# Grouping the RWKV output products behind the state products, with a two-bank PSUM tile

## The chip, the cores and the metric

The kernel runs on one core of a Trainium2 chip. The metric is the device time of one execution in microseconds (us); of several runs the median is given. The engines are named as the profile names them: PE (TensorE, matmul; PEld is its weight load), DVE (VectorE), ACT (ScalarE), POOL (GpSimd) and SP (SyncE, which only issues transfers here). Matmul results land in PSUM, which has eight banks of 512 f32 in each of 128 partitions.

## The reference, cut to what matters

One layer of a hybrid encoder: a normalised input goes through one projection into three head groups (Mamba-2 SSD, RWKV-7, memory cross-attention), whose outputs are joined, projected, normalised and added to the input. Sequence 4096, width 1024, all f32. The change lies in the RWKV group, four heads of 64:

```python
def rwkv7_recurrence(r, w, k, v, a_vec, b_vec):
    """S_t = S_{t-1} (diag(w_t) + a_t^T b_t) + v_t^T k_t ; y_t = S_t r_t."""
    ...

def rwkv7_group(u, mu, w0, w2, a0, a2, k_k, k_a, r_k, lnx_w, lnx_b):
    prev = jnp.pad(u, ((0, 0), (1, 0), (0, 0)))[:, :l, :]
    us = (u + (prev - u) * mu).astype(jnp.float32)        # token shift
    r, k, v, g = ...                                      # 256 columns each, then two low-rank inputs
    ...
    y = rwkv7_recurrence(rh, hs(decay), kh, vh, -kk, kk * ah)
    mean = jnp.mean(y, axis=-1, keepdims=True)
    var = jnp.mean(jnp.square(y - mean), axis=-1, keepdims=True)
    y = (y - mean) * lax.rsqrt(var + LNX_EPS)
    ...
    return ((y + bonus).reshape(b, l, W) * jax.nn.silu(g)).astype(u.dtype)
```

## The kernel before

The kernel has three phases: `phase_a` (SSD group, to about 800 us of the span), `phase_b` (RWKV group, about 800 to 1610 us) and `phase_c` (cross-attention and output projection). In each the sequence is cut into 16 pieces of 256 tokens; this text calls the work on one piece in phase B a round. Matrix products of the projections are split into high and low parts, so each takes three matmuls a block of 128 inputs (`proj_cm`, L143).

In phase B several generators are traced in turn by `weave`, which gives each a share: `stage1` of piece i (projections and what is made of them), `gram2` and `solve2` of piece i-1, `stage3` and `stage4` of piece i-2. Each `yield` hands over to the next generator. The order of tracing is the priority; a planner with its own timing model then lays the instructions of each engine in order, taking among those that are ready the one traced first. `tc.high_priority(offset=n)` treats what is traced inside as if it had been traced n places earlier; `tc.issue_after(x)` lets nothing traced inside go ahead of x on x's engine. The engines then run their instructions in the planned order, with semaphores between engines.

- `shifted` projects a block pair into the PSUM tile `ps_pj` (two of these), and evicts it with the token shift: ACT scales by 1-mu into `tt` (L583), DVE adds mu times the column before (L584), POOL puts the last token of the piece before into column 0 (L586, from `cm`), and DVE writes the new last token into `cm` (L587). There are nine blocks in five calls a round.
- `gram2` makes four 128x128 products for each of two heads, twice a round (L746), into the PSUM banks `ps_yd` and `ps_st`, and DVE evicts each bank under a mask into `AT` (L749). In the last round the banks `ps_g` and `ps_tr` are used.
- `solve2` inverts 64x64 triangular blocks, with small matmuls (L801, L809, L821, L831); `nct` (L762, L769) is an intermediate of it, `N` the next.
- `tokmaj` copies v, the scaled b and k, `rr` (the scaled r, L856, ACT) and `el` (L857, POOL) of the next piece into the layouts that `stage3` reads.
- `stage3` runs four chunks of 64 tokens, one after the other. A chunk copies the state `ST` into `UV` (L887), multiplies (L894), copies to `X` (L897), multiplies (L901), copies to `UV` (L906), multiplies into the state's update (L911) and adds it (L914); `S0` is the decayed state (L889, POOL). After each second chunk the output products of both are made: from `rr` and the states (L928), and from `AT` and `UV` (L931), into the banks `ps_yd` and `ps_st` again. These are f32 products on 64 rows or columns (64x64 and 128x64 shapes of the array); the profile counts two matmuls for each.
- `stage4` takes mean (L943), difference (L947) and variance of the outputs, transposes them back, and writes the piece to DRAM.

The order in which TensorE gets the output products is thus the planner's: a product may go as soon as its inputs are there.

## Time and profile before

| what | value |
|---|---|
| time, median of 3 runs | 2216.97 us (2215.18 to 2217.18) |
| the profiled execution | 2213.0 us, its span 2211.3 us, granted TensorE clock 0.99 |
| PE busy | 2151.4 us, 97% |
| DVE / ACT / POOL busy | 1502.5 (68%) / 1184.0 (54%) / 721.5 us (33%) |
| DMA | 97 GB/s over the span |
| one round of phase B in its steady part | 46.6 us |

A row of the timeline has the start in us from the beginning of the span, the duration in us, the engine, the line, the operation, what is written and read (by the program's tile names), the form, and how many alike were merged. For a matmul the form gives the part of the array that is used (rows x columns), then what streams through. Rows of groups have a count after x, busy us in all, the mean ns of one, and after the bar the idle time of that engine just before them, with what ended it.

### The profile page before, as it was taken

Reading aid. Unit: us, or ns where it says so; the run is one execution under the profiler, and the core shown is the slowest. Engines: PE = TensorE matmul, PEld = TensorE weight load, DVE = VectorE, ACT = ScalarE, POOL = GpSimd, SP = SyncE. Lnnn points to the kernel's source line nnn. Section 1 sums busy time; section 2 is a strip of 40 time slices with the busy share of each in tenths; the row PEclk is TensorE's granted clock in tenths of the full one; section 3 lists DMA queues with packets and bytes.
Section 4 is the critical chain, followed back from the end, with each engine's and each line's share of the span. In section 5 each row is a group of like instructions: output and inputs, shape, how many; then the busy total and the mean of one; then the engine's idle time right before and its main releaser. Section 6 shows DMA issues by size and latency. Waiting matters only on the chain.

```text
span 2211.3 us, 51042 instructions
## 1 busy us (share of the span) xinstructions
PE 2151.4 (97%) x20705; PEld 1980.4 (90%) x20705; DVE 1502.5 (68%) x3438; ACT 1184.0 (54%) x2877; POOL 721.5 (33%) x1043
## 2 busy tenths in 40 slices
PE   6999999999999889999999999999999999999998
PEld 6999999999999888899899998898888888888986
DVE  6788878888888886577776777777664444444452
ACT  7555555555554565566666666677643333333441
POOL 1334344343443343233334334333112212222223
PEclk9999999999999999999999999999999999999999
DMA  6332223322233331112111121123253324333232
GB/s 206 128 113 96 87 96 123 117 96 92 94 137 120 108 96 40 44 45 83 49 45 45 45 80 47 49 73 135 92 189 117 133 102 162 110 130 133 101 124 77
DMA packets 83610, 218.86 MB, mean 99 GB/s; under 512 B 9191, under 2 KB 45486, under 8 KB 71086
## 3 DMA queue, kind: packets, MB, share of 16 engines
q1 hardware_dynamic: 81294, 215.56, 27.9%
q8 instruction: 163, 2.67, 0.5%
q14 instruction: 73, 0.60, 0.1%
q10 hardware_dynamic: 2080, 0.04, 0.1%
HBM read 152.00 MB, written 63.57 MB: 97 GB/s over the span
## 4 chain that ended last, share of the span: by engine, by line
PE 85%; DMA 5%; DVE 5%; ACT 3%; issue 1%; POOL 1%; POOLq 0%; SPq 0%; ACTq 0%; DVEq 0%
PE ps_pj L143 40%; PE ps_pj L153 8%; PE ps_yd L153 8%; PE ps_st L153 7%; DMA w_st<-in_w_in_dram 1%; DVE cc L312 1%; PE ps_yd L441 1%; PE ps_yd L746 1%; PE ps_pj L1159 1%; PE ps_tr L132 1%; PE ps_yo L894 1%; PE ps_yo L901 1%; PE ps_tr L1147 1%; PE ps_st L433 1%; PE ps_yo L911 1%
## 5 line engine op out<-in xcount | busy, mean ns | idle before, releaser
L143 PE MATMUL ps_pj<-hh,w_hi 128*128 128x256 f32 x2704 | 792.6, 293 | 13.4 <-ACT w_hi L80 3.8
L143 PE MATMUL ps_pj<-hh,w_lo 128*128 128x256 f32 x2704 | 780.9, 289 | 1.6 <-DVE w_lo L81 1.6
L143 PE MATMUL ps_pj<-hl,w_hi 128*128 128x256 f32 x2704 | 778.8, 288 | 0.0
L143 PEld LDWEIGHTS ps_pj<-hh,w_hi 128*128 128x128 f32 x2704 | 521.0, 193 | 25.9 <-ACT w_hi L80 7.3
L143 PEld LDWEIGHTS ps_pj<-hh,w_lo 128*128 128x128 f32 x2704 | 520.7, 193 | 8.5 <-DVE w_lo L81 2.6
L143 PEld LDWEIGHTS ps_pj<-hl,w_hi 128*128 128x128 f32 x2704 | 521.1, 193 | 6.8
L312 DVE SCALAR_TENSOR_TENSOR cc<-ux,cwh,cc 128x256 f32<-128x256 f32 x384 | 218.0, 611 | 11.4 <-ACT cc L309 11.0
L153 PE MATMUL ps_pj<-w_hi,hh 128*128 128x260 f32 (+1 forms) x528 | 153.5, 291 | 4.8 <-ACT hh L135 4.0
L153 PE MATMUL ps_pj<-w_hi,hl 128*128 128x260 f32 (+1 forms) x528 | 150.9, 286 | 0.0
L153 PE MATMUL ps_pj<-w_lo,hh 128*128 128x260 f32 (+1 forms) x528 | 149.9, 284 | 0.0
L1166 DVE TENSOR_TENSOR ya<-ps_pj,ya 64x256 f32<-64x256 f32 x64 | 27.0, 422 | 117.5 <-ACT ya L1165 117.2
L153 PEld LDWEIGHTS ps_pj<-w_hi,hh 128*128 128x128 f32 x528 | 99.9, 190 | 6.9 <-ACT hh L135 4.4
L1193 POOL TENSOR_TENSOR sq<-sq 128x1 f32<-128x1 f32 x32 | 6.3, 196 | 306.1 <-ACT ot L1191 306.1
L1199 POOL TENSOR_TENSOR xr<-ot,xr 128x512 f32<-128x512 f32 x64 | 89.8, 1426 | 44.5 <-DVE ot L1198 44.5
L153 PEld LDWEIGHTS ps_pj<-w_lo,hh 128*128 128x128 f32 x528 | 100.1, 190 | 0.4 <-DVE w_lo L81 0.2
L153 PEld LDWEIGHTS ps_pj<-w_hi,hl 128*128 128x128 f32 x528 | 99.9, 189 | 0.0
L153 PE MATMUL ps_yd<-wo0h,yh 128*128 128x512 f32 x248 | 98.4, 397 | 1.2 <-DVE ot L1198 1.2
L153 PE MATMUL ps_st<-wo1h,yh 128*128 128x512 f32 x248 | 97.6, 394 | 1.0 <-ACT wo1h L1259 1.0
L153 PE MATMUL ps_st<-wo1l,yh 128*128 128x512 f32 x248 | 97.6, 394 | 0.0
L153 PE MATMUL ps_st<-wo1h,ylo 128*128 128x512 f32 x248 | 97.4, 393 | 0.0
L153 PE MATMUL ps_yd<-wo0h,ylo 128*128 128x512 f32 x248 | 97.3, 392 | 0.0
L153 PE MATMUL ps_yd<-wo0l,yh 128*128 128x512 f32 x248 | 97.2, 392 | 0.0
(470 smaller groups left out, 5095.5 us busy)
## 6 DMA issues: line engine op xcount, KB each, us to landing
hl<-hTd SPq DMA_DIRECT2D x32, 1024.0 KB
hh<-hTd SPq DMA_DIRECT2D x32, 1024.0 KB
xt<-in_x_dram SPq DMA_DIRECT2D x32, 512.0 KB
hTd<-hh SPq DMA_DIRECT2D x16, 1024.0 KB
hTd<-hl SPq DMA_DIRECT2D x16, 1024.0 KB
R<-rowd SPq DMA_DIRECT2D x32, 512.0 KB
xr<-in_x_dram SPq DMA_DIRECT2D x32, 512.0 KB
out_dram<-xr SPq DMA_DIRECT2D x32, 512.0 KB
```

The source lines that it names most:

```text
L132: te.transpose(pt[:, q * P:(q + 1) * P], src[:, k * P:(k + 1) * P], ident)
L143: te.matmul(outp, lhsT=a[:, k, :], rhs=b[:, k, :], start=(n == 0), stop=(n == 3 * KB - 1))
L153: te.matmul(outp, lhsT=a[:, k, tsl], rhs=b[:, k, 0:ncol], start=(n == 0), stop=(n == 3 * KB - 1))
L312: v.scalar_tensor_tensor(out=cc[:, b_, :], in0=ux[:, b_, j:j + NT], scalar=wj(j), in1=cc[:, b_, :], op0=ALU.mult, op1=ALU.add)
L433: te.matmul(pst[:, gr * 256:gr * 256 + 256], lhsT=q[c]["btm"][:, gr * P:(gr + 1) * P], rhs=q[c]["xde"][:, gr * 256:gr * 256 + 256], start= ...
L441: te.matmul(yd[hf * 64:hf * 64 + 64, h * 64:h * 64 + 64], lhsT=R[:, h, hf * 64:hf * 64 + 64], rhs=xdt[:, h * 64:h * 64 + 64], start=True, ...
L746: te.matmul(pa[:, c_ * P:(c_ + 1) * P], lhsT=BK[hs, p_, c_].rearrange("p a t -> p (a t)"), rhs=AR[hs, p_, c_].rearrange("p a t -> p (a t)" ...
L894: te.matmul(pch[hs, p_ * C:p_ * C + C], lhsT=AT[:, pc, h, 0:C], rhs=UV[:, pc, h, :], start=True, stop=True)
L901: te.matmul(pch[hs, 128 + p_ * C:128 + p_ * C + C], lhsT=TT[hs, pc].rearrange("p a t -> p (a t)"), rhs=X[hs, p_, :], start=True, stop=True)
L911: te.matmul(pch[hs, 256 + p_ * C:256 + p_ * C + C], lhsT=BKt[:, pc, hs], rhs=UV[:, pc, h, :], start=True, stop=True)
L1166: v.tensor_tensor(out=ya[hs], in0=pg[hs], in1=ya[hs], op=ALU.add)
L1199: g.tensor_tensor(out=xr[:, cs], in0=ots[n_], in1=xr[:, cs], op=ALU.add)
```

## The change

`ps_yd` and `ps_st` move from the common PSUM pool into a pool of two banks of their own, opened anew for each phase. In phase B these two banks are one tile, `two`. `gram2` evicts both banks with one DVE instruction (except in the last round); `stage4` takes the mean and the difference with one instruction each. The output products are traced under `issue_after` the last state product (L911) of the pair. The evictions of `shifted` are traced at a priority raised by 300 places; the new last token goes to the other one of two tiles `cm0`, `cm1`, ahead of POOL's addition. The copy into `rr` moves from ACT to POOL, and `nct` shares its place with `N`.

```diff
+    psx = []
+    def two_banks():
+        stack = ExitStack()
+        psx.append(stack.enter_context(tc.tile_pool(name=f"ps{len(psx)}", bufs=1, space=bass.MemoryType.PSUM)))
+        return stack
     def psum(tag, bufs):
-        return ps.tile([P, 512], F32, name="ps_" + tag, tag=tag, bufs=bufs)
+        return (psx[-1] if tag in ("yd", "st") else ps).tile([P, 512], F32, name="ps_" + tag, tag=tag, bufs=bufs)
...
-        cm = bs.tile([P, 9], F32, name="cm")
-        v.memset(cm, 0.0)
+        cm2 = [bs.tile([P, 9], F32, name=f"cm{n_}") for n_ in range(2)]
+        v.memset(cm2[0], 0.0)
+        cms = {m0: tuple(cm2) for m0 in range(9)}
...
         def shifted(hT, ws, m0, nm, mid=None, pool=None, at=0, tag=None):
+            co, cn = cms[m0]
+            cms[m0] = (cn, co)
...
-            for b_ in range(nb):
-                s.activation(out=tt[:, b_, :], ...)
-                v.scalar_tensor_tensor(out=us[:, b_, 1:NT], ...)
-            g.tensor_tensor(out=us[:, :, 0], in0=tt[:, 0:nb, 0], in1=cm[:, m0:m0 + nb], op=ALU.add)
-            v.tensor_tensor(out=cm[:, m0:m0 + nb], in0=pv[:, :, NT - 1], in1=mu[:, m0:m0 + nb], op=ALU.mult)
+            with tc.high_priority(offset=300):
+                for b_ in range(nb):
+                    s.activation(out=tt[:, b_, :], ...)
+                    v.scalar_tensor_tensor(out=us[:, b_, 1:NT], ...)
+                v.tensor_tensor(out=cn[:, m0:m0 + nb], in0=pv[:, :, NT - 1], in1=mu[:, m0:m0 + nb], op=ALU.mult)
+            g.tensor_tensor(out=us[:, :, 0], in0=tt[:, 0:nb, 0], in1=co[:, m0:m0 + nb], op=ALU.add)
...
+        two = lambda: psx[-1].tile([P, 2, 512], F32, name="ps_two", tag="two", bufs=1)
         def gram2(i, r):
...
-                pas = (psum("g", 1), ps_tr()) if i == NS - 1 else (psum("yd", 1), psum("st", 1))
+                big = None if i == NS - 1 else two()
+                pas = (psum("g", 1), ps_tr()) if big is None else (big[:, 0, :], big[:, 1, :])
...
-                for h, pa in enumerate(pas):
-                    v.tensor_tensor(out=AT[:, p_ * NC_:(p_ + 1) * NC_, h, :], in0=pa..., op=ALU.mult)
-                    yield
+                if big is None:
+                    ...
+                else:
+                    v.tensor_tensor(out=AT[:, p_ * NC_:(p_ + 1) * NC_].rearrange("p x h t -> p h x t"),
+                                    in0=big.rearrange("p h (x t) -> p h x t", t=P),
+                                    in1=amask.unsqueeze(1).unsqueeze(1).broadcast_to([P, 2, NC_, P]), op=ALU.mult)
+                yield
+                yield
...
-            s.copy(out=rr[:, :, cs, :], in_=AR[:, :, cs, 1, :])
+            g.tensor_copy(out=rr[:, :, cs, :], in_=AR[:, :, cs, 1, :])
...
         def stage3(i, r, nxt=None):
-            pys = [psum("yd", 1), psum("st", 1)]
+            py = two()
...
-                        te.matmul(pch[hs, 256 + p_ * C:256 + p_ * C + C], lhsT=BKt[:, pc, hs], rhs=UV[:, pc, h, :],
+                        upd = te.matmul(pch[hs, 256 + p_ * C:256 + p_ * C + C], lhsT=BKt[:, pc, hs], rhs=UV[:, pc, h, :],
...
                 if c_ % 2 == 1:
-                    for step in range(2):
-                        ...
-                                    yo = pys[h][par * 64:par * 64 + 64, o:o + C]
+                    with tc.issue_after(upd.ins):
+                        for step in range(2):
+                            ...
+                                        yo = py[par * 64:par * 64 + 64, h, o:o + C]
...
         def stage4(i, r):
-            pys = r["py"]
+            pyv = r["py"][:, :, 0:256].rearrange("p h (c t) -> p h c t", t=C)
...
-            for h in range(2):
-                v.tensor_reduce(out=mean[:, h, :], in_=pys[h][:, 0:256]..., axis=AX.X, op=ALU.add)
+            v.tensor_reduce(out=mean, in_=pyv, axis=AX.X, op=ALU.add)
...
-            for h in range(2):
-                v.tensor_tensor(out=yc[:, h::2, :], in0=pys[h][:, 0:256]..., op=ALU.subtract)
+            v.tensor_tensor(out=yc.rearrange("p (c h) t -> p h c t", h=2), in0=pyv,
+                            in1=mean.unsqueeze(3).broadcast_to([P, 2, 4, C]), op=ALU.subtract)
```

In `solve2`, `nct` is now made with the tag of `N`, and each phase opens its pair of banks with `two_banks()`.

## The prediction

> **What bounds the kernel now.** I read the page first, then busy time by stage, then the chain and the waits of TensorE, and last the timeline of TensorE through one round of the RWKV stage. A round is 256 tokens; there are 16.

> ```profile
> PE 2151.4 (97%) x20705; PEld 1980.4 (90%) x20705; DVE 1502.5 (68%) x3438; ACT 1184.0 (54%) x2877; POOL 721.5 (33%) x1043
> ...
> 1001.00:1420.00 419.00, 419.00 (x5686) 377.12 (x5686) 299.73 (x792) 277.68 (x684) 161.99 (x216) 1.00 0.14 53
> ...
> 1500.00:1600.00 100.00, 92.79 (x1150) 82.94 (x1150) 69.00 (x169) 65.99 (x164) 22.65 (x37) 0.97 0.33 115
> ...
> L769 DVE STREAM_TRANSPOSE t<-nct x10: 711/711/712, 1009.8 to 1429.2; 128x512 f32<-128x512 f32 x10
> ```

> The columns of the two middle rows are the stretch, its length, then busy us of PE, PEld, DVE, ACT and POOL, and the granted clock. From 1001 to 1420 us TensorE is busy in all 419.00 us at clock 1.00, DVE in 72% and ACT in 66%. L769 runs once a round: ten of them from 1009.8 to 1429.2, nine intervals, so a round is 46.6 us. There TensorE is the bound and every us of another engine is free while TensorE has work. From 1500 to 1600 TensorE is short of work for 7.2 us. So the change must be read in TensorE's own stream, where a matmul's busy time overlaps its neighbour's; the distance between starts is what counts. The timeline of one round:

> ```profile
> 1195.65 0.28 PE L143 MATMUL ps_pj<-hh,w_hi 128*128 128x256 f32 x1
> 1195.77 0.28 PE L143 MATMUL ps_pj<-hl,w_hi 128*128 128x256 f32 x1
> ...
> 1195.98 0.33 PE L928 MATMUL ps_yd<-ST,rr 64*64 64x64 f32 x2
> ...
> 1196.46 0.28 PE L143 MATMUL ps_pj<-hh,w_hi 128*128 128x256 f32 x1
> ...
> 1196.93 0.28 PE L143 MATMUL ps_pj<-hl,w_hi 128*128 128x256 f32 x1
> ...
> 1197.14 0.27 PE L928 MATMUL ps_st<-ST,rr 64*64 64x64 f32 x1
> ...
> 1197.53 0.33 PE L931 MATMUL ps_yd<-UV,AT 128*64 128x64 f32 x2
> ...
> 1198.13 0.28 PE L143 MATMUL ps_pj<-hh,w_hi 128*128 128x256 f32 x1
> ...
> 1204.60 0.28 PE L143 MATMUL ps_pj<-hh,w_hi 128*128 128x256 f32 x1
> 1204.81 0.45 PE L931 MATMUL ps_yd<-UV,AT 128*64 128x64 f32 x6
> ...
> 1205.40 0.28 PE L143 MATMUL ps_pj<-hh,w_lo 128*128 128x256 f32 x1
> ...
> 1206.00 0.28 PE L143 MATMUL ps_pj<-hl,w_hi 128*128 128x256 f32 x1
> 1206.21 0.45 PE L911 MATMUL ps_yo<-UV,BKt 128*64 128x64 f32 x8
> 1206.49 0.40 PE L931 MATMUL ps_st<-UV,AT 128*64 128x64 f32 x6
> ...
> 1207.04 0.28 PE L143 MATMUL ps_pj<-hh,w_hi 128*128 128x256 f32 x1
> ...
> 1212.87 0.28 PE L143 MATMUL ps_pj<-hl,w_hi 128*128 128x256 f32 x1
> 1213.07 0.27 PE L928 MATMUL ps_yd<-ST,rr 64*64 64x64 f32 x1
> ...
> 1213.56 0.28 PE L143 MATMUL ps_pj<-hh,w_hi 128*128 128x256 f32 x1
> ...
> 1218.96 0.27 PE L928 MATMUL ps_yd<-ST,rr 64*64 64x64 f32 x1
> ...
> 1219.23 0.45 PE L894 MATMUL ps_yo<-UV,AT 128*64 128x64 f32 x8
> ...
> 1219.62 0.27 PE L928 MATMUL ps_yd<-ST,rr 64*64 64x64 f32 x1
> ...
> 1219.88 0.33 PE L931 MATMUL ps_yd<-UV,AT 128*64 128x64 f32 x2
> ...
> 1220.26 0.44 PE L809 MATMUL ps_g<-Dt,pw 32*32 32x16 f32 x32
> ```

> Two projection products (128*128) start 0.12 apart (1195.65, 1195.77). When a group of small products (64*64 or 128*64) stands between them, the first one after it comes late, and so does the second. So I measure a group from the last projection product before it to the second one after it, less 2 x 0.12. L931 x6 alone: 1205.40 - 1204.60 - 0.24 = 0.56. L911 x8 with L931 x6: 1207.04 - 1206.00 - 0.24 = 0.80. Eight more products cost 0.24, 0.03 each; so the group as such costs 0.56 - 0.18 = 0.38, more than its products. L928 x4 alone: 1213.56 - 1212.87 - 0.24 = 0.45; L928 x2 alone: 1196.46 - 1195.77 - 0.24 = 0.45. At 0.02 a product these groups cost 0.37 and 0.41. A change of shape inside a group is cheaper: L894 x8 between L928 takes 1219.62 - 1219.23 = 0.39, 0.15 over its eight products.

> **The change, part by part.**

> *State and output products as one group.* Today the output products (L928, L931) start whenever their inputs are there, apart from the state products (L911). In the new kernel none of a pair of chunks may start on TensorE before the last L911 of the pair; by then ST, rr and UV are all there, since the last L911 reads the last UV. They stand next in program order, so I expect L911 x8, L928 x16, L931 x16 in one run, twice a round. Removed per round: L928 x2 alone 0.41; L928 x14 with L931 x4, 1198.13 - 1196.93 - 0.24 = 0.96 less 14 x 0.02 and 4 x 0.03, 0.56; L931 x6 alone 0.38; L928 x4 alone 0.37; and in the mixed group from 1218.96 to 1220.26 five changes of shape become two, 3 x 0.15 = 0.45. Sum 2.17. Added: L911 to L928 to L931 in both groups, 4 x 0.15 = 0.60. Net 1.57 us a round if all of it joins. Not all need do: where L894 stood between two sets of L928 (1219.23), the order showed that a recurrence product can come between. I take a fifth off: 1.25. Ends: 0 (nothing joins) and 1.57. Ten steady rounds give 12.5; in the six at the ends of the stage TensorE is partly idle, so I count half there, 6 x 0.63 = 3.8. Together 16.3, between 0 and 25 (16 x 1.57). Nobody waits for the delayed output products but the token-major copies of the next round (UV, rr) and the mean, and L911 itself no longer stands behind them.

> The other parts, with the rows of their engines:

> ```profile
> L749 DVE TENSOR_TENSOR AT<-ps_yd,amask 128x512 f32<-128x512 f32 x30 | 20.6, 686 | 17.4 <-PE ps_yd L746 17.0 <-PE ps_st L746 0.3
> ...
> L379 DVE TENSOR_TENSOR R<-R,acs 128x1024 f32<-128x1024 f32 x32 | 39.8, 1242 | 0.0
> ...
> L587 DVE TENSOR_TENSOR cm<-ps_pj,pcol 128x2 f32<-128x2 f32 (+1 forms) x80 | 11.7, 146 | 6.0 <-POOL ur L586 6.0
> ...
> L583 ACT ACTIVATE tt<-ps_pj,omu 128x256 f32<-128x256 f32 x144 | 67.7, 470 | 30.0 <-PE ps_pj L143 18.6 <-DVE uv L584 7.6 <-POOL uk L660 1.5
> ...
> L856 ACT COPY rr<-AR 128x256 f32<-128x256 f32 x32 | 12.9, 406 | 0.0
> ...
> L889 POOL TENSOR_TENSOR S<-ST,el 128x128 f32<-128x128 f32 x64 | 31.5, 492 | 137.6 <-DVE ST L914 125.1 <-DVE T L782 10.0 <-issue 2.3
> ...
> L660 POOL TENSOR_TENSOR uk<-uk,m 128x512 f32<-128x512 f32 x16 | 20.6, 1287 | 52.8 <-ACT thw L659 44.4 <-issue 4.8 <-ACT X L897 3.6
> ...
> 1234.61 0.68 DVE L749 TENSOR_TENSOR AT<-ps_st,amask 128x512 f32<-128x512 f32 x1
> ...
> 1236.90 0.48 PE L746 MATMUL ps_yd<-AR,BK 64*128 64x128 f32 x2
> ```

> *One gram eviction of two banks.* 30 pairs of 0.69 and 0.68 become 30 of about 1.24 (L379, same width): 0.13 each, 4 us of DVE in all, off the path, since DVE is idle in 28% of the steady stretch. The mean and its subtraction lose one instruction each per round in the same way. Worth 0. Its risk is a wait: one tile of two banks is free only when the whole eviction is done. Today the second eviction ends at 1235.29 and the next gram half starts at 1236.90, with projection products between, so 1.6 us of cover; gone, it costs up to 1.24 a hand-over.

> *Token shares double-buffered.* DVE's carry no longer waits for POOL's read of the old one: 6.0 us of DVE idle go, in 80 places. It now stands ahead of POOL's addition and frees ps_pj sooner. TensorE's steady stretch shows no idle, so 0 there; at most the same 6.0 at the ends of the stage.

> *Projection evictions 300 places earlier.* 144 on ACT of 0.47, as many on DVE, 80 carries. Queued behind them on ACT and DVE are the recurrence's small copies, each later by up to one eviction. A chunk has 11.6 us (46.6 / 4), so a few delays of 0.47 have room. I take 0, between -4 and +4: each group of small products that a new order splits off or joins is worth 0.38 either way, and ten of them in the whole stage are 4 us.

> *rr from ACT to POOL.* 32 copies of 0.41 leave ACT (13 us). On POOL, between L889 (0.49 for 128 columns) and L660 (1.29 for 512, two inputs); nearest by width is L889, so I take 0.65, 21 us. POOL is busy in 162 of 419 us, and rr is wanted only in the next round: 0. Waiting for L928, it holds POOL's queue; behind it stands L889, whose product is wanted only two products later.

> *nct in N's place, psum pools per phase.* nct is written a round after N's last use; the new pools begin where the old banks are already read out: 0.

> The profiled execution took 2213.0 us (span 2211.3 and 1.7 around it), 4.0 under the median 2217.0. The sum, -16.3, is taken from its rows; put on the median it gives 2201 us.

> **The rivals.**

> *The products join only in part* (older projection products come between, each leaving a lone group of 0.38): half the gain, -8, 2209. For it: the split at 1219.23. Against: at 1206.21 L911 and L931 that were ready together ran together.

> *It moves nothing that shows.* The new order splits other small groups: three or four more a round at 0.38 eat 1.25. For it: raising 368 evictions changes the whole order, and gram, solve and recurrence groups stand apart by chance. 2217.

> *Slower: the two-bank tile.* Three hand-overs a round (gram, gram, output products) go through one tile. If two a round expose their 1.24 to TensorE, 2.48 go against 1.25: +1.23 in 13 rounds' worth, 16, so 2233. It decides from one exposed hand-over a round. Against it: the 1.6 us of cover above, and output products that now come later, after their banks were read.

> *Slower: POOL's copy holds up DVE.*

> ```profile
> 1213.37 2.78 POOL L663 TENSOR_TENSOR BK<-uk,lw 64x512 f32<-64x512 f32 x2
> ...
> 1213.53 1.58 DVE L665 TENSOR_TENSOR AR<-ur,E 128x512 f32<-128x512 f32 x1
> ...
> L679 DVE TENSOR_TENSOR AR<-thw,E 128x512 f32<-128x512 f32 x16 | 10.9, 679 | 0.0
> ```

> L665 runs beside POOL and takes 1.58; L679, same shape, takes 0.68. If each rr copy held DVE for its 0.65 and TensorE waited for that every time, 2 x 0.65 x 16 = 21 come back: 2222. Against: DVE has 28% to spare. [...]

> **How the numbers follow.** No change that can be told is within 0.2%, 4.4 us. Full gain (2193 to 2208, likeliest 2201): 0.60. Part of it, 2209: 0.14. Nothing, 2217: 0.13. Two-bank wait, 2233: 0.08. POOL, 2222: 0.05. Faster 0.74, same 0.13, slower 0.13. The range goes from 25 off (2192) with 1 us of run spread, 2191, to 2222; outside lie the two-bank case and little below.

> **What would show it.** Right: a steady round of 45.3 us by the same transposes; L928 and L931 after L911 without projection products between; L749 30 times at 1.24; no idle of the carry by POOL; TensorE still busy throughout. Wrong: lone L928 or L931 groups left; more groups elsewhere with a round of 46.6; idle of TensorE before L746 or L928 put down to AT; L665-like stretching on DVE with TensorE idle behind it.

## The result and the profile after

| | before | after |
|---|---|---|
| median of the runs | 2217.07 us (2215.18 to 2222.49) | 2251.43 us (2248.63 to 2253.92, 4 runs) |
| ratio to before, 95% interval | 1 | 1.016 (1.0147 to 1.0173) |
| span of the profiled execution | 2211.3 us | 2252.2 us, granted clock 0.978 |

The kernel became slower by 34 us, where 16 less were forecast. The counterparts of the rows shown of before come first: the page, the busy time by stage (stretch, length, busy us of PE, PEld, DVE, ACT and POOL, granted clock), the groups of instructions, and the answer for one line. The lines have new numbers: L143 is now L151, L583 to L587 are L596 to L600 (the carry is L599, ahead of POOL's L600), L746 is L762, L749 is L769, L769 is L792, L911 is L934, L928 is L952, L931 is L955, and the copies of `tokmaj` are L872 to L887.

```profile
PE 2143.1 (95%) x20705; PEld 1976.1 (88%) x20705; DVE 1511.2 (67%) x3376; ACT 1172.7 (52%) x2845; POOL 740.2 (33%) x1075
...
1001.00:1420.00 419.00, 398.06 (x5425) 361.79 (x5424) 294.99 (x726) 261.93 (x642) 163.31 (x223) 0.98 0.14 53
1500.00:1600.00 100.00, 89.53 (x1152) 80.04 (x1151) 73.49 (x188) 69.54 (x167) 25.32 (x42) 0.93 0.31 100
```

```profile
L762 PE MATMUL ps_two<-AR,BK 64*128 64x128 f32 x480 | 43.5, 296 | 1.4 <-DVE AT L769 1.3
L769 DVE TENSOR_TENSOR AT<-ps_two,amask 128x1024 f32<-128x1024 f32 x30 | 36.6, 1219 | 8.5 <-PE ps_two L762 8.3
L879 POOL COPY rr<-AR 128x256 f32<-128x256 f32 x32 | 13.1, 408 | 21.4 <-PE ps_two L952 20.8
L599 DVE TENSOR_TENSOR cm<-ps_pj,pcol 128x2 f32<-128x2 f32 (+1 forms) x80 | 11.9, 149 | 0.0
...
L792 DVE STREAM_TRANSPOSE t<-nct x9: 711/714/715, 1024.2 to 1411.3; 128x512 f32<-128x512 f32 x9
```

The same 419 us of the steady stretch, in which TensorE had been busy throughout, now hold 398.06 us of it: 20.9 us of idle, and 261 matmuls fewer. L792 runs nine times from 1024.2 to 1411.3, eight intervals, so a round takes 48.4 us instead of 46.6. The gram eviction has the size that was forecast (30 times 1.22), the copy of `rr` on POOL costs 0.41 and not 0.65, the carry (L599) waits for nothing any more, and the two-bank tile makes a gram product wait 1.3 us in the whole kernel.

The waits of TensorE in the steady stretch of after (engine, what it was to write, its line, what it waited for; us in all, times, longest) are these; in the same stretch of before the list is empty:

```profile
PE ps_tr L872 <- ACT UV L876: 11.1, 7, 1.6
PE ps_pj L151 <- DVE cm L599: 8.1, 14, 1.0
PE ps_yo L924 <- ACT X L920: 1.6, 7, 0.2
```

None of them is a wait for the two-bank tile or for the copy of `rr`; L599, the carry, belongs to the evictions that were raised. The timeline of one round shows how they come about; TensorE, ACT and DVE are mixed in it:

```profile
1160.23 0.48 DVE L597 SCALAR_TENSOR_TENSOR uk<-ps_pj,pcol,tt 128x255 f32<-128x255 f32 x1 [0.50 <-ACT tt L596]
...
1166.81 0.71 DVE L792 STREAM_TRANSPOSE t<-nct 128x512 f32<-128x512 f32 x1 [1.52 <-ACT nct L785]
...
1170.59 0.46 ACT L596 ACTIVATE tt<-ps_pj,omu 128x256 f32<-128x256 f32 x1
...
1175.77 0.28 PE L151 MATMUL ps_pj<-hh,w_lo 128*128 128x256 f32 x1
1175.97 0.45 PE L934 MATMUL ps_yo<-UV,BKt 128*64 128x64 f32 x8
1176.36 0.46 PE L952 MATMUL ps_two<-ST,rr 64*64 64x64 f32 x16
1176.75 0.69 PE L955 MATMUL ps_two<-UV,AT 128*64 128x64 f32 x16
1177.36 0.39 PE L663 MATMUL ps_tr<-sqh,hones 128*128 128x256 f32 x1
...
1177.74 0.62 ACT L910 COPY UV<-ST 64x128 f32<-64x128 f32 x2 [0.68 <-DVE ST L937]
1178.09 0.48 DVE L597 SCALAR_TENSOR_TENSOR ur<-ps_pj,pcol,tt 128x255 f32<-128x255 f32 x1 [0.30 <-PE ps_tr L663]
1178.09 0.76 PE L917 MATMUL ps_yo<-UV,AT 128*64 128x64 f32 x8
1178.38 0.91 ACT L810 ACTIVATE t<-T,lm 128x256 f32<-128x256 f32 x2
1179.32 1.11 ACT L876 COPY UV<-ps_tr 64x128 f32<-64x128 f32 x4
1180.48 0.44 PE L872 MATMUL ps_tr<-ident,uv 128*128 128x128 f32 x2 [1.62 <-ACT UV L876]
1181.58 0.48 PE L924 MATMUL ps_yo<-X,TT 64*64 64x64 f32 x8 [0.23 <-ACT X L920]
1181.94 0.48 DVE L597 SCALAR_TENSOR_TENSOR ur<-ps_pj,pcol,tt 128x255 f32<-128x255 f32 x1 [1.91 <-ACT tt L596]
1182.34 0.15 DVE L599 TENSOR_TENSOR cm<-ps_pj,pcol 128x2 f32<-128x2 f32 x1
1182.64 0.55 PE L151 MATMUL ps_pj<-hh,w_hi 128*128 128x256 f32 x1 [0.57 <-DVE cm L599]
```

The grouping itself came out as forecast: L934 x8, L952 x16 and L955 x16 stand in one run. But after the last projection product at 1175.77 TensorE has no projection left to put between the small ones: both `ps_pj` tiles are full. One of them holds r: ACT's part of its first eviction is over at 1171.05, but DVE's starts 7.0 us later, at 1178.09. It writes `ur`, whose place `sqh` holds until L663 has read it, and L663 stands behind the group of small products. In before the same step took 1.5 us, in a_onebank (below) 3.0. L872 waits 1.62 us for a bank of `ps_tr`, which ACT empties (L876) only behind a copy of the recurrence (L910) and a scaling in the solve (L810). L924 waits for X behind that, and the next projection for the evictions of r (L597, L599), of which the second comes 3.9 us after the first. Together 2.42 us in this round.

The reason can be read one step earlier, from k's evictions. In after the first eviction of k stands at 1160.23, 6.6 us ahead of the transpose of `nct` (1166.81); in before it stood 5.3 us behind it:

```profile
1196.20 0.71 DVE L769 STREAM_TRANSPOSE t<-nct 128x512 f32<-128x512 f32 x1
1201.45 0.48 DVE L584 SCALAR_TENSOR_TENSOR uk<-ps_pj,pcol,tt 128x255 f32<-128x255 f32 x1
```

So in after the projections run some 12 us further ahead of the solve than before, and by about as much ahead of the recurrence: this eviction stands 36.0 to 38.1 us ahead of the last state update (L937) of the piece two earlier in six of eight rounds, and stood 24.7 us ahead in before (L914). TensorE's filler is used up early in the round, and the small dependent products are left over with nothing between them.

The dry spots also cost clock. The same stretch by windows, with the granted clock behind POOL's busy time:

```profile
1137.50:1178.46 40.96, 40.56 (x598) 37.00 (x596) 29.78 (x76) 25.66 (x62) 12.00 (x21) 1.00 0.16 60
1178.46:1181.87 3.41, 1.56 (x20) 1.19 (x20) 1.45 (x3) 3.29 (x11) 2.57 (x3) 1.00 0.00 0
1181.87:1188.70 6.83, 6.26 (x72) 5.78 (x72) 2.69 (x8) 1.29 (x4) 4.88 (x5) 0.50 0.00 0
1188.70:1228.00 39.30, 39.13 (x561) 35.89 (x554) 29.19 (x75) 25.37 (x61) 11.79 (x20) 1.00 0.17 62
```

After 3.41 us in which TensorE was busy for 1.56, the clock was 0.50 for 6.83 us. This happens four times between 1001 and 1420 (twice for 6.83 us, twice for 3.41), 20.5 us in all. At half speed that loses at most 10.2 us (TensorE also waits in part of it). All four lie in the eight rounds below: 1.28 us a round.

The account of a steady round, summed over eight rounds of the trace: 48.39 us, of which 2.61 are waits of TensorE over 0.1 us. 48.39 - 2.61 - 1.28 = 44.5 us, which is what the change would have given with TensorE kept busy; 45.3 was forecast. The first transposes of `nct` already come late: the first at 830.2 us against 820.6, the fourth at 975.5 against 963.1, so 12 us are lost up to there (3.7 of them stand already at the stage's first eviction of k), 24 in the eleven rounds that follow, and 1 at the stage's end (last difference of the outputs at 1644.3 against 1607.3).

### The profile page after: what moved, and what is told of

It is laid out like the page before. It is cut to its first block, busy times and chain, and to the rows that moved or that the text cites. A ratio compares the mean times of both kernels' runs of the same rounds, so it can differ in the third digit from the quotient of the medians.

```text
span 2252.2 us, 51042 instructions
## 1 busy us (share of the span) xinstructions
PE 2143.1 (95%) x20705; PEld 1976.1 (88%) x20705; DVE 1511.2 (67%) x3376; ACT 1172.7 (52%) x2845; POOL 740.2 (33%) x1075
## 4 chain that ended last, share of the span: by engine, by line
PE 75%; DVE 11%; DMA 6%; ACT 5%; issue 3%; POOL 1%; SPq 0%; POOLq 0%; DVEq 0%; ACTq 0%
PE ps_pj L151 35%; PE ps_yd L161 7%; PE ps_st L161 7%; PE ps_pj L161 7%; DVE cc L320 2%; PE ps_two L762 1%; DMA R<-rowd 1%; PE ps_pj L1181 1%; PE ps_tr L1169 1%; PE ps_yd L449 1%; PE ps_yo L934 1%; PE ps_tr L140 1%; DMA w_st<-in_w_in_dram 1%; DMA xt<-in_x_dram 1%; PE ps_st L441 1%
## 5 line engine op out<-in xcount | busy, mean ns | idle before, releaser
L151 PE MATMUL ps_pj<-hh,w_hi 128*128 128x256 f32 x2704 | 794.6, 294 | 20.1 <-DVE cm L599 13.2
L151 PE MATMUL ps_pj<-hh,w_lo 128*128 128x256 f32 x2704 | 780.6, 289 | 4.5 <-DVE w_lo L89 4.3
L151 PE MATMUL ps_pj<-hl,w_hi 128*128 128x256 f32 x2704 | 779.9, 288 | 0.0
L151 PEld LDWEIGHTS ps_pj<-hh,w_hi 128*128 128x128 f32 x2704 | 525.7, 194 | 32.5 <-ACT Dt L817 9.0
L151 PEld LDWEIGHTS ps_pj<-hh,w_lo 128*128 128x128 f32 x2704 | 525.2, 194 | 9.9 <-DVE w_lo L89 6.5
L151 PEld LDWEIGHTS ps_pj<-hl,w_hi 128*128 128x128 f32 x2704 | 525.5, 194 | 5.1
L596 ACT ACTIVATE tt<-ps_pj,omu 128x256 f32<-128x256 f32 x144 | 68.0, 472 | 60.7 <-PE ps_pj L151 34.6
```

Of the source, the lines that this page charges most:

```text
L151: te.matmul(outp, lhsT=a[:, k, :], rhs=b[:, k, :], start=(n == 0), stop=(n == 3 * KB - 1))
L596: s.activation(out=tt[:, b_, :], in_=pv[:, b_, :], func=AF.Copy, scale=omu[:, m0 + b_:m0 + b_ + 1])
```

## The experiments

The first theory after the result: TensorE runs dry because the plan has moved the projections ahead, and what costs is the idle and the clock. Its rivals: the two-bank tile costs by its hand-over, the raised evictions by what queues behind them, the copy on POOL by holding up others, the grouping by delaying the readers of `UV`. Two marks are read from each trace: the waits of TensorE over 0.1 us per round, and where k's first eviction stands from the transpose of `nct` (minus is ahead; the usual value, or a range). After was timed beside a before of 2217.07 us, the others beside one of 2211.7 to 2213.0; so a difference to after is taken from the ratios below.

| kernel | median us | ratio to before (95%) | steady round us | waits us a round | k's eviction |
|---|---|---|---|---|---|
| before | 2211.7 to 2213.0 beside these | 1 | 46.59 | 0 | +5.3 |
| after | 2251.43 | 1.016 (1.0147 to 1.0173) | 48.39 | 2.61 | -6.6 |
| a_noraise | 2229.9 | 1.007 (1.005 to 1.009) | 48.17 | 2.37 | -7.8 |
| a_nogroup | 2231.77 | 1.0076 (1.0052 to 1.0099) | 47.46 | 0.86 | changing, -3.7 to +2.2 |
| a_rract | 2230.8 | 1.0086 (1.0068 to 1.0105) | 47.10 | 2.24 | -3.6 |
| a_onebank | 2185.72 | 0.988 (0.9863 to 0.9897) | 44.53 | 0 | +4.1 |
| b_group | 2202.05 | 0.995 (0.9931 to 0.9969) | 45.49 | 0.54 | changing, one of eight at -7.0 |
| b_raise | 2207.21 | 0.9975 (0.9965 to 0.9986) | 45.97 | 0 | +5.3 |
| b_two | 2207.3 | 0.9975 (0.9961 to 0.9989) | 46.19 | 0.47 | +0.6 to +4.6 |
| b_rr | 2210.68 | 0.9995 (0.9986 to 1.0005) | 46.70 | 0 | +5.2 |
| b_group_raise | 2197.92 | 0.9929 (0.9907 to 0.9951) | 44.55 | 0 | +4.1 |
| b_two_group | 2208.42 | 0.9989 (0.9975 to 1.0003) | 46.77 | 0.98 | changing, -6.5 to +4.1 |
| b_two_raise | 2221.32 | 1.0038 (1.0022 to 1.0055) | 47.67 | 0.97 | changing, -6.8 to +3.7 |
| b_two_rr | 2194.52 | 0.9922 (0.9905 to 0.9939) | 45.31 | 0 | +4.3 |
| a_twoevict | 2231.77 | 1.0097 (1.0079 to 1.0116) | 47.94 | 2.43 | -2.9 to -7.6 |
| a_off100 | 2229.01 | 1.0078 (1.0061 to 1.0095) | 48.18 | 2.25 | -7.8 |
| a_gate | 2206.99 | 0.998 (0.9968 to 0.9991) | 45.31 | 0.34 | +1.9 |
| o_lead | 2408.37 | 1.0884 (1.0864 to 1.0905) | 59.0 | 7.80 | -14 to -21 |

Names beginning with a_ start from the kernel after, those with b_ from the one before; o_lead starts from a_onebank.

The steady rounds can be set against each other once their waits, and what the lower clock lost (the round times one less its granted clock), are taken off. The ten kernels with the order rule, o_lead aside, then come to 43.6 to 45.4 us, after to 44.5; the seven without it come to 45.3 to 46.7, a_nogroup to 46.0. So the gain of the grouping is in after too, and waits and clock take it away.

**One part of after undone.** a_noraise traces the evictions of `shifted` at their own place again:

```diff
-            with tc.high_priority(offset=300):
+            with ExitStack():
```

> The changed kernel with the evictions of the projections at their own priority again; all else as changed. Theory R (the raised evictions let the projections run ahead of the norm products, whose operand holds the buffer of ur; then both ps_pj tiles are full, TensorE runs dry once a round and its clock drops): the dry spots go, a round is 45.3 to 46 us, time 2198 to 2210. Theory G (the group of 40 small products itself holds up the next chunk and the token-major copies, and TensorE runs dry for that): no change, 2245 to 2255.

2229.9 us, in neither range, with k's eviction still 7.8 us ahead in most rounds and TensorE dry for 2.37 us a round. The raised evictions are not the cause of the dry spots, though without them after is faster by 0.9%, some 20 us.

a_nogroup takes the order rule of the output products away:

```diff
-                    with tc.issue_after(upd.ins):
+                    with ExitStack():
```

> The changed kernel without the rule that the output products go behind the last state product; evictions stay raised. Theory R: the dry spots stay and the gain of the grouping is lost too, 2250 to 2270. Theory G: the dry spots go, about the time of before, 2210 to 2220.

2231.77 us, again in neither range. TensorE still waits, 0.86 us a round, and there are 17.1 groups of small products a round again instead of 13.8 (counted as runs between products of the shape 128*128). The waits fall by two thirds: the grouping deepens the dry spots, but it is not all of their cause.

a_rract puts the copy of `rr` back on ACT:

```diff
-            g.tensor_copy(out=rr[:, :, cs, :], in_=AR[:, :, cs, 1, :])
+            s.copy(out=rr[:, :, cs, :], in_=AR[:, :, cs, 1, :])
```

> The changed kernel with the copy into rr on ACT again. Theory P: 2195 to 2210. Theories T and C: 2240 to 2260, or a few us more for the 13 us that ACT takes back.

2230.8 us, in neither range: by the ratios 16 us less, but the waits are there (2.24 us a round).

a_onebank replaces the two-bank tile by the two banks of before, with two evictions and two instructions each for the mean and the difference; all else is as in after:

```diff
-            py = two()
+            pys = [psum("yd", 1), psum("st", 1)]
```

> The changed kernel with the gram products, output products, mean and difference in two banks of their own tiles again, one DVE instruction a bank; grouping, raised evictions and rr on POOL stay. Theory T (the two-bank tile is what costs: one hand-over for gram, gram and output products): 2192 to 2205, a round of about 45 us and no dry spot. Theory P (the copy into rr on POOL costs): 2240 to 2255. Theory C (grouping and raised evictions only hurt together): 2235 to 2255.

2185.72 us: by the ratios 2.8% of before, 62 us, under after, and 1.2% under before (0.988, 0.9863 to 0.9897), 6 below the range of theory T and the fastest kernel of this study. Its steady stretch, and then rows of the timeline of one round:

```profile
1001.00:1420.00 419.00, 418.91 (x5880) 383.53 (x5880) 322.09 (x840) 285.05 (x704) 172.31 (x244) 1.00 0.14 53
```

```profile
1137.32 0.71 DVE L785 STREAM_TRANSPOSE t<-nct 128x512 f32<-128x512 f32 x1
1141.45 0.47 DVE L597 SCALAR_TENSOR_TENSOR uk<-ps_pj,pcol,tt 128x255 f32<-128x255 f32 x1
...
1150.91 0.45 PE L910 MATMUL ps_yo<-UV,AT 128*64 128x64 f32 x6
...
1154.46 0.28 PE L151 MATMUL ps_pj<-hh,w_hi 128*128 128x256 f32 x1
1154.58 0.38 PE L865 MATMUL ps_tr<-ident,uv 128*128 128x128 f32 x2
```

TensorE is busy in 418.91 us of 419.00 at clock 1.00. L865 here is the product that waited in after (L872 there): between the recurrence product ahead of it and itself stand 28 projection products, 3.4 us of work. The wait that it would have is gone behind them. Of the 70 us between the profiled executions of after and a_onebank 46 lie in the eleven rounds from the fourth transpose of `nct` to the fifteenth, and 16 ahead of them.

**One part added to before.** b_group gives before only the order rule of the output products:

```diff
+                    with tc.issue_after(upd.ins):
                         for step in range(2):
```

> The kernel before with one edit: the output products behind the last state product. Theory R: the grouping alone gives its gain of about 1.25 us a round, 2197 to 2208. Theory G: the dry spots appear here too, 2235 to 2255.

2202.05 us, 11 less; the groups fall from 18.0 to 15.9 a round and the round by 1.1 us, though TensorE waits 0.54 us a round here, most of it in the one round of eight where k's eviction comes first.

b_raise gives before the raised evictions, the two tiles `cm0` and `cm1`, and `nct` in N's place, which makes room for them:

```diff
+            with tc.high_priority(offset=300):
                 for b_ in range(nb):
```

> The kernel before with raised evictions and the two tiles of token shares (and nct in N's place, to make room), nothing else. Theory R: dry spots as in the changed kernel, without the gain of the grouping, 2240 to 2265. Theory G: no change, 2210 to 2222.

2207.21 us, 6 less, where theory G had no change and theory R far more; TensorE is busy throughout and the groups stay at 18.0 a round.

b_two gives before the two-bank tile with its single evictions, the pools and `nct` in N's place:

```diff
-            pys = [psum("yd", 1), psum("st", 1)]
+            py = two()
```

> The kernel before with the two-bank tile and its single evictions (and nct in N's place, the pools of two banks); no grouping, no raised evictions, rr on ACT. Theory T: 2228 to 2245, TensorE dry after the gram products or the output products. Theories P and C: 2212 to 2220.

2207.3 us, 5 less and below both ranges. The tile by itself costs no time, though TensorE waits 0.47 us a round with k's eviction behind the transpose in all of them.

b_group_raise joins the grouping and the raised evictions, on one-bank tiles and with `rr` on ACT:

> The kernel before with the grouping and the raised evictions (and two tiles of token shares, nct in N's place), nothing else. Theory C: 2235 to 2255, dry spots as in the changed kernel. Theories T and P: the two gains of 11 and 6 us add, 2193 to 2202.

2197.92 us; the steady round is 44.55, as in a_onebank, from which it differs by the copy of `rr` and the pools; that difference of 12 us lies outside the steady stretch.

**The two-bank tile with one other part.** These ask whether a certain pair does the harm.

```diff
 # b_two_group:  b_two plus the order rule
+                    with tc.issue_after(upd.ins):
 # b_two_raise:  b_two plus the raised evictions
+            with tc.high_priority(offset=300):
 # b_two_rr:     b_two plus the copy on POOL;   b_rr: before plus it
-            s.copy(out=rr[:, :, cs, :], in_=AR[:, :, cs, 1, :])
+            g.tensor_copy(out=rr[:, :, cs, :], in_=AR[:, :, cs, 1, :])
```

> Kernel before with the two-bank tile and the output products behind the state products, nothing raised, rr on ACT. Theory (the tile does harm only where the plan lays k's eviction ahead of nct's transpose, and that needs the tile together with another part): the planned order is mixed here, with k ahead in some rounds, so the gain of the grouping (1.0 us a round) is partly lost: 2200 to 2220, with idle of TensorE only in the rounds with k ahead. Rival (the tile simply costs by itself beside any regrouping): all rounds the same and longer than 46.6 us, 2225 or more. Rival (parts simply add up): 2207 less 11, 2196.

> Kernel before with the two-bank tile and the raised evictions, products not grouped, rr on ACT. Theory: the plan has k ahead in some rounds, so 2205 to 2225, with TensorE idle in those rounds. Rival (parts add up): 2207 less 6, 2201. Rival (raising is what does the harm): as a_nogroup, 2232, in every round.

> Kernel before with the two-bank tile and rr's copy on POOL; no raise, no grouping. The plan keeps k's eviction behind nct's transpose throughout. Theory: no harm, 2200 to 2210 and no idle of TensorE to speak of. Rival (the copy on POOL together with the two-bank tile is what costs 20 us, by whatever way): 2220 or more.

> Kernel before with only rr's copy on POOL instead of ACT. The prediction's step: 0, that is 2213 within 4. Rival (DVE held up by POOL's copy): up to 21 us more, 2222 or later. Rival (ACT freed lets the recurrence's copies go sooner, as 2198 against 2186 between the two one-bank kernels with and without it suggests): 2200 to 2205.

b_two_group 2208.42, b_two_raise 2221.32, b_two_rr 2194.52, b_rr 2210.68. The copy on POOL costs nothing alone and gains 13 us beside the tile; so in these kernels POOL is not what holds up the others; 2194.52 is below both ranges. The raised evictions beside the tile lose 14 us; their groups rise to 18.4 a round, and TensorE waits 0.97 us. That leaves some 0.6 us of the 1.70 by which its round is longer than that of b_raise without a cause shown. b_two_group lies between: the gain of the grouping is gone. It is the kernel to look at, for its rounds come in a pattern of four and can be compared inside one trace. In three of the four k's eviction stands 4.1, 4.1 and 0.6 us behind the transpose, and TensorE waits 0, 0 and 0.2 us; in the fourth it stands 6.5 ahead, and TensorE waits 3.95 us (3.44 in the next such round). The latter round in the timeline, and then the waits of TensorE in the whole steady stretch:

```profile
1091.72 0.48 DVE L593 SCALAR_TENSOR_TENSOR uk<-ps_pj,pcol,tt 128x255 f32<-128x255 f32 x1 [0.46 <-ACT tt L592]
1098.19 0.71 DVE L788 STREAM_TRANSPOSE t<-nct 128x512 f32<-128x512 f32 x1 [1.56 <-ACT nct L781]
```

```profile
PE ps_yo L930 <- ACT UV L925: 2.7, 3, 1.0
PE ps_tr L868 <- ACT UV L872: 2.1, 2, 1.1
PE ps_yo L920 <- ACT X L916: 1.2, 2, 0.6
PE ps_yo L913 <- ACT UV L906: 1.2, 2, 0.6
```

The waits fall in the rounds where k comes first, but for 0.2 us in each of the rounds at 0.6. Taken over all kernels but o_lead, eight rounds each from the sixth transpose on, 136 rounds (those of one kernel are much alike): in 54 k's first eviction stands ahead of the transpose, and TensorE waits 2.48 us a round on the mean (0.47 to 3.95; mean length 47.6 us). In 82 it stands behind, and TensorE waits 0.13 us on the mean and 1.8 us at most, in 68 of them not at all (mean length 45.9 us).

**What of the tile matters.** a_twoevict keeps the two-bank tile but evicts each bank with an instruction of its own, and takes the mean and the difference likewise:

```diff
+                    for h, pa in enumerate(pas):
+                        v.tensor_tensor(out=AT[:, p_ * NC_:(p_ + 1) * NC_, h, :], in0=pa..., op=ALU.mult)
...
```

> The changed kernel with the two-bank tile kept, but read by one DVE instruction a bank again (gram eviction, mean, difference). Theory L: the tile's hand-over as a unit stays, the planned order still has k ahead, 2230 to 2255. Theory S (the single wide DVE instructions are what shifts the order): 2185 to 2205.

2231.77 us, with k's eviction ahead and 2.43 us of waits a round. So the one wide instruction is not the cause of the dry spots, though the kernel with two is by the ratios 14 us faster.

a_off100 raises the evictions by 100 places instead of 300 (2229.01 us, k's eviction ahead):

> The changed kernel with the evictions raised by 100 places instead of 300. Theory L: the planned order still has k ahead of the gram products, so 2228 to 2250. Theory X (the planned order is a lottery, any small edit may give 2190 or 2250): anything, with dry spots that don't go with the lead of k.

Its steady round and its waits (48.18 and 2.25 us) are those of a_noraise (48.17 and 2.37): raised by 100 places the evictions cost nothing more, raised by 300 they cost 18 us.

**The order itself.** a_gate leaves after as it is, but lets the second block of k's projection go on TensorE only behind the last gram product of the second half:

```diff
+                        with tc.issue_after(gm["g"]):
+                            if next(gen, gen) is gen:
...
```

> The changed kernel with one more rule of order: the second block of the k projection of a round goes on TensorE behind the second gram half of that round; all else as changed. Theory L (the two-bank tile alters the planner's order so that the k projection stands ahead of the gram products, the projections lead by several us all round, and TensorE's queue then holds products whose PSUM tile or input isn't ready): the lead and the dry spots go although the two-bank tile stays, 2185 to 2200. Theory H (the hand-over of the two-bank tile itself keeps TensorE waiting): no gain, 2240 to 2260.

2206.99 us, 7 above the range of theory L: by the ratios 40 of the 62 us between after and a_onebank come back, by one rule of order and with every other instruction of after in place. k's eviction now stands 1.9 us behind the transpose, the waits fall from 2.61 to 0.34 us a round, and the round is 45.31; that this is the value forecast for after is chance, since 0.34 of it are waits. The rows of one round, and the steady stretch:

```profile
1192.06 0.71 DVE L804 STREAM_TRANSPOSE t<-nct 128x512 f32<-128x512 f32 x1 [2.65 <-ACT nct L797]
...
1193.94 0.48 DVE L607 SCALAR_TENSOR_TENSOR uk<-ps_pj,pcol,tt 128x255 f32<-128x255 f32 x1 [0.32 <-ACT tt L606]
```

```profile
1001.00:1420.00 419.00, 416.19 (x5820) 380.65 (x5819) 304.08 (x773) 278.62 (x687) 168.52 (x240) 1.00 0.15 55
```

o_lead goes the other way: a_onebank, whose order is good, with the whole of `stage1` (the projections and what is made of them) raised by 300 places.

```diff
-weave(..., (chain(*back, stack(r1)), 26), (first, 30),
+weave(..., (chain(*back, stack(r1)), 26), (first, 30, 300),
...
```

> The kernel with one-bank tiles and grouping, raised evictions and rr on POOL (2186 in the run above), with the whole stream of projections traced at a priority raised by 300 places, which puts k ahead of the gram products. Theory L: the dry spots appear without the two-bank tile, 2220 to 2250. Theory H: none, 2183 to 2195.

2408.37 us, 158 above the range of theory L. Its projections lead by 14 to 21 us, and the steady stretch and the costliest waits in it are:

```profile
1001.00:1420.00 419.00, 362.74 (x4447) 326.63 (x4446) 242.22 (x618) 215.01 (x524) 132.63 (x184) 0.84 0.11 41
```

```profile
PE ps_yo L927 <- ACT UV L922: 17.3, 13, 4.4
PE ps_tr L878 <- issue: 7.5, 3, 2.5
```

56 us of idle in 419, clock 0.84, on one-bank tiles. A lead of the projections is enough to run TensorE dry; the two-bank tile isn't needed for it. The lead here is two to three times that of after, and the longest waits are others, so this run gives the sign and not the size.

## Why the prediction was wrong

*TensorE stays the bound.* This is the step that failed. "There TensorE is the bound and every us of another engine is free while TensorE has work" held for the order of before. I carried it over to an order that the change was to lay anew. Each term was then priced with projection products as cover between the small ones, and nothing in the sum asked whether they would still stand there. With k's projections 12 us further ahead they did not, and that cost 2.61 us of waits and up to 1.28 us of clock a round. The parts do add up to a gain one by one: by their ratios b_group, b_raise, b_two and b_rr give 0.5, 0.25, 0.25 and 0.05%, 23 us together; joined they lose 34.

*"Projection evictions 300 places earlier: 0, between -4 and +4".* The bounds were made of lone groups (0.38 us each) and saw neither side: -6 alone (b_raise), -4 beside the grouping (b_group_raise against b_group), +14 beside the two-bank tile (b_two_raise against b_two), +20 in after (a_noraise, by the ratios). A change of priority has no price of its own; it has one for each order that it joins.

*State and output products as one group: 1.25 us a round, -16 in all.* Right in mechanism, about right in size. Alone it took 1.1 us off the round and 11 off the kernel (b_group); beside the raised evictions 1.42 off the round (45.97 to 44.55) and 9 off the kernel. All of the output products of after stand behind L934, as "what would show it" asked, and the groups fell to 13.8 a round.

*"Nobody waits for the delayed output products but the token-major copies of the next round."* Those copies are L876, and L872 waits for them: the reader was named, and then passed over because it had cover. With projections left (a_onebank) it costs nothing; without them it was the longest wait of the round.

*Two-bank tile.* The rival gave the right sign by the wrong mechanism. A hand-over of 1.24 us was to be exposed twice a round; 1.3 us were, in the whole kernel. The tile alone gains 5 us (b_two). It matters by changing the order: with the other parts k's projections come ahead.

*The copy on POOL.* 0.41 us against 0.65 estimated, alone 0 as forecast (b_rr 0.9995, 0.9986 to 1.0005); in company it was not 0, but 13 us of gain beside the tile (b_two_rr) and 16 us of loss in after (a_rract). The rival that it holds up DVE does not hold in b_two_rr, which is faster with it (2194.52 us against the 2207.3 of b_two). L665 took 1.58 us in before (median of its 16) and, as L678, 0.69 in after (its longest 1.67); no run here shows that the longer ones cost the kernel time.

*Gram eviction, carry, `nct`, pools.* The gram eviction and the carry came as forecast (1.22 us; no idle of DVE before the carry). `nct` in its new place and the pools were not run by themselves.

*The wrong signs.* "Idle of TensorE before L746 or L928 put down to AT" was listed and did not come, but for 1.3 us in the whole kernel; the idle stands before L872, L924 and L151. "TensorE still busy throughout" was the sign that answered.

Not settled: why the plan takes k ahead with the two-bank tile and another part, and with one-bank tiles in only one round of those counted (b_group); the 21 us that a_gate still lacks to a_onebank; and why four separate parts of after (the raise, the grouping, the copy on POOL, the one wide eviction) each give 14 to 20 us back when undone, with waits still there. By the transposes of `nct` in their profiled executions, 9 to 13 us of it lie in the eleven rounds from the fourth to the fifteenth, and 5 to 10 ahead of the fourth; what shortens the filling no run took apart.

## What to carry to other kernels

Where a planner lays the order, price a change of priority, of tiles or of an order rule first by what it does to the order: before trusting a sum of parts, ask which filler stands between the dependent products, and how far it may run ahead. A busy engine in the profile of before tells that its cover was well placed, not that it can't be used up. Two marks, the waits of the bound engine in a steady stretch and the place of one eviction against a fixed point of the round, sorted most rounds of this study (b_two waits a little with the eviction behind); and parts that gain one by one should be timed together, and again without each.

## What the runs showed of the hardware

In after short waits cost more than their length. In its steady stretch no single wait was longer than 1.6 us, but where they came together TensorE was busy for 1.56 us of 3.41 and the granted clock was 0.50 for the next 6.83 us. It lasted 3.41 us after another such stretch:

```profile
1130.68:1134.09 3.41, 1.59 (x16) 1.25 (x17) 1.50 (x5) 2.96 (x10) 3.33 (x3) 1.00 0.00 0
1134.09:1137.50 3.41, 3.41 (x18) 3.41 (x17) 1.44 (x3) 0.60 (x2) 3.33 (x4) 0.50 0.00 0
```
